# First attention of an encoder: one reciprocal for two blocks' sums, and a lower rate of filling products

## The chip, the cores and the metric

The kernel runs on one core of a Trainium2 chip. The metric is the device time of one execution in microseconds (us), from its first instruction to its last. Names of engines: PE is the matrix engine (PEld its weight load), DVE the vector engine, ACT the scalar engine, POOL the GpSimd engine, SP the engine that issues most DMAs. Lines such as L1004 are lines of the kernel before; the change's own lines stand in its diff.

## The reference, cut to what matters

A two-layer encoder over 512 tokens of width 1024, float32 throughout, is computed. The first layer's attention has two groups of eight heads; both use the same softmax attention:

```python
def one(qblk):                                  # a block of 128 queries
    sc = einsum('bkgqd,bksd->bkgqs', qblk, kt) * scale
    p = softmax(sc, axis=-1)
    return einsum('bkgqs,bksd->bkgqd', p, vt)
```

Group A has 64-wide queries and keys; group B has 96-wide ones that come from low-rank latents. Their outputs are joined and pass through one projection, then an MLP follows; the second layer has a neighbourhood attention and another MLP, then a final norm.

## The kernel before, in words

Float32 accuracy is had by splitting each operand into a high and a low part and adding three products (`mm3`, L500 to L503; two passes for group A's scores). So a weight chunk is loaded by SP (L190), copied to its high part by ACT (L212, L222) and its low part is made by DVE or POOL (L202).

The change lies in `attend` (L961 to L1022), which treats 16 heads of 4 blocks, thus 64 blocks of 128 queries, numbered 0 to 63 below. Blocks 0 to 31 are group A, 32 to 47 the first half of group B, 48 to 63 its second half. One block goes through these steps:

- scores: two (A) or three (B) matmuls of 128x512 into a PSUM bank `s`, of which there are two (L997);
- row maximum: a DVE instruction that writes the scaled scores to a tile `p` in SBUF, with the maximum in a column (L1001). There are five buffers `p`;
- exponential on ACT, with the sum of the row into another column (L1003);
- one reciprocal on DVE (L1004), and one scaling of `p` by it on POOL (L1005);
- three blocks later in program order: four transposes on PE into a bank `t`, of which there are two (L972), the copy of the high part by ACT (L974), and the low part by DVE (L975);
- for each two blocks: eight value matmuls (L985), four by the high parts and four by the low parts in turn. At a head's end ACT and DVE fold the two halves of the output (L946, L949), and for each two heads the result is split (L833 on ACT, L830 on DVE).

Between blocks `fill.run(1.5)` in `step` (L1088) emits other products, called filling products here: generators that each report an estimated duration (0.69 for an `mm3`), of which so many are emitted that 1.5 us more are used up. During group A these are the projections to the latents (L1090 to L1093), the latents' norm, and queries, keys and values of B's first half (`projB`, L838; L850, L878, and L907 to L909 for the values). From block 35 on they are parts of the output projection (L1084 to L1087) and B's second half. `fill.until` (L1044) emits all that is left of a half's projections before its first block, since that block reads them.

This gives the program's order only. The instructions of this stage are then ordered by a scheduler, which decides for each engine what comes first (the second layer's attention has an order written out by hand, the first has not). So a rate changed in one line moves rows on all engines.

## Time and profile before

| | |
|---|---|
| median of 3 runs | 1183.46 us (1182.31 to 1184.22) |
| profiled execution, first to last instruction | 1184.0 us |
| PE busy | 1160.5 us, 98% |
| DVE busy | 883.2 us, 75% |
| ACT busy | 640.3 us, 54% |
| POOL busy | 526.1 us, 44% |
| first scores of the stage that is changed | at 68.95 us |
| last transposes of the stage | at 247.17 us |

No time around the span is given for the profiled execution; its span lies among the three runs, 0.5 us over their median. A matmul's duration in the trace overlaps the next one's, so what one costs on PE is read from the start of one row to the start of the next. The same holds for DVE and ACT.

### The profile page before, as it was taken

The page shows a single profiled execution, that of the slowest core. Times are in us where ns is not written, and L with a number is a line of the kernel's source. Part 1 is how long each engine was busy: PE and PEld are TensorE (multiplying, and loading weights), DVE is VectorE, ACT ScalarE, POOL GpSimd, SP SyncE. Part 2 cuts the span into 40 slices and gives each one's busy share as a digit, 9 for nine tenths or more (in the row PEclk, how much of TensorE's full clock was granted, in tenths as well). Part 3 has the DMA queues.
Part 4 walks back from the last instruction along what each step waited for, and adds up shares of the span by engine and source line. Part 5 has one row for each costly group of instructions (what it writes and reads, how often), then busy time and mean ns, then how long its engine had stood idle before and what let it go on. Part 6 is the DMA issues. An engine that isn't in the chain of part 4 may idle for free.

```text
span 1184.0 us, 19784 instructions
## 1 busy us (share of the span) xinstructions
PE 1160.5 (98%) x7128; PEld 1021.2 (86%) x7128; DVE 883.2 (75%) x1514; ACT 640.3 (54%) x1081; POOL 526.1 (44%) x662
## 2 busy tenths in 40 slices
PE   9989999999999999999999999999999999999997
PEld 8667778888899899988998998988889989998895
DVE  5788998878967368786884676667996736778975
ACT  4468676664546247562553565555554624666344
POOL 3267343224562377819602232231376625774710
PEclk9999999999999999999999999999999999999998
DMA  7223225212524723225226464433352341322412
GB/s 244 71 54 92 68 78 134 62 56 77 167 86 134 263 70 90 72 90 165 67 72 178 131 184 126 116 112 109 107 165 76 115 134 55 98 64 89 143 36 71
DMA packets 110145, 128.01 MB, mean 108 GB/s; under 512 B 9075, under 2 KB 86816, under 8 KB 110048
## 3 DMA queue, kind: packets, MB, share of 16 engines
q1 hardware_dynamic: 106992, 119.30, 33.5%
q0 software_dynamic: 2304, 6.31, 2.2%
q8 instruction: 56, 0.92, 0.3%
q10 hardware_dynamic: 752, 1.15, 0.3%
q14 instruction: 41, 0.34, 0.1%
HBM read 104.32 MB, written 6.29 MB: 93 GB/s over the span
## 4 chain that ended last, share of the span: by engine, by line
PE 81%; DVE 4%; ACT 1%; issue 1%; POOL 0%; DVEq 0%; ACTq 0%
PE mm L503 8%; PE mm L501 8%; PE mm L502 8%; PE mm L390 4%; PE mm L389 4%; PE mm L388 4%; PE t L388 3%; PE t L389 3%; PE t L390 3%; PE s L502 2%; PE s L503 2%; PE s L501 2%; PE s L390 2%; PE s L388 2%; PE s L389 2%; PE s L997 2%
## 5 line engine op out<-in xcount | busy, mean ns | idle before, releaser
L309 DVE TENSOR_TENSOR wlo<-a,whi 128x896 fp32r<-128x896 f32 x132 | 161.8, 1230 | 83.7 <-ACT whi L308 82.9
L308 ACT ACTIVATE whi<-a 128x896 fp32r<-128x896 f32 x132 | 125.0, 950 | 155.0 <-PE o L502 45.8
L501 PE MATMUL mm<-a,whi 128*128 128x512 f32 x485 | 195.9, 406 | 0.9 <-DVE a L915 0.7
L503 PE MATMUL mm<-a,wlo 128*128 128x512 f32 x485 | 192.1, 397 | 2.5 <-DVE wlo L202 2.5
L502 PE MATMUL mm<-a,whi 128*128 128x512 f32 x485 | 192.5, 397 | 0.1
L202 DVE TENSOR_TENSOR wlo<-raw,whi 128x1024 fp32r<-128x1024 f32 (+4 forms) x117 | 139.3, 1193 | 66.4 <-ACT whi L212 63.9
L212 ACT ACTIVATE whi<-raw 128x1024 fp32r<-128x1024 f32 (+3 forms) x120 | 116.4, 971 | 92.2 <-PE s L502 39.8
L302 POOL TENSOR_TENSOR a<-a 128x128 f32<-128x128 f32 x132 | 85.1, 645 | 173.3 <-DMA a<-in_ffn_w_up_dram 103.9
L303 POOL TENSOR_TENSOR a<-a 128x256 f32<-128x256 f32 x132 | 120.2, 910 | 10.3
L304 POOL TENSOR_TENSOR a<-a 128x128 f32<-128x128 f32 x132 | 115.1, 872 | 10.3
L503 PEld LDWEIGHTS mm<-a,wlo 128*128 128x128 f32 x485 | 91.7, 189 | 23.7 <-DVE wlo L202 3.4
L501 PEld LDWEIGHTS mm<-a,whi 128*128 128x128 f32 x485 | 91.8, 189 | 20.4 <-PE t L972 0.9
L502 PEld LDWEIGHTS mm<-a,whi 128*128 128x128 f32 x485 | 91.9, 190 | 17.4 <-DVE a L545 0.4
L388 PE MATMUL mm<-a,whi 128*128 128x256 f32 x370 | 103.9, 281 | 0.0
L389 PE MATMUL mm<-a,whi 128*128 128x256 f32 x370 | 103.9, 281 | 0.0
L390 PE MATMUL mm<-a,wlo 128*128 128x256 f32 x370 | 103.7, 280 | 0.0
L1005 POOL TENSOR_SCALAR p<-p,ti 128x512 f32<-128x512 f32 x64 | 46.2, 724 | 92.3 <-DVE ti L1004 81.1
L1430 POOL TENSOR_SCALAR p<-p,ti 128x256 f32<-128x256 f32 x64 | 35.6, 567 | 104.8 <-DVE ti L1429 91.8
L388 PE MATMUL t<-a,whi 128*128 128x256 f32 x264 | 74.2, 281 | 0.0
L389 PE MATMUL t<-a,whi 128*128 128x256 f32 x264 | 74.1, 281 | 0.0
L390 PE MATMUL t<-a,wlo 128*128 128x256 f32 x264 | 73.9, 280 | 0.0
L390 PEld LDWEIGHTS mm<-a,wlo 128*128 128x128 f32 x370 | 69.6, 188 | 0.2 <-DVE wlo L309 0.2
(338 smaller groups left out, 3210.8 us busy)
## 6 DMA issues: line engine op xcount, KB each, us to landing
a<-in_ffn_w_up_dram SPq DMA_DIRECT2D x104, 256.0 KB
raw<-in_ffn_w_down_dram SPq DMA_DIRECT2D x46, 512.0 KB
raw<-in_od_w_qkv_dram SPq DMA_DIRECT2D x64, 128.0 KB
a<-in_ffn_w_down_dram SPq DMA_DIRECT2D x28, 256.0 KB
raw<-in_ffn_w_up_dram SPq DMA_DIRECT2D x12, 512.0 KB
raw<-in_ev_w_in_dram SPq DMA_DIRECT2D x12, 384.0 KB
a<-a SPq DMA_DIRECT2D x18, 256.0 KB
bias<-bx SPq DMA_DIRECT2D x16, 256.0 KB
```

The source lines that it names most:

```text
L202: z = lambda: (eng or DVE).tensor_tensor(to, src, f32(high), op=ALU.subtract)
L212: ACT.activation(hi[:, 0:m], raw[:, 0:m], AF.Copy)
L303: POOL.tensor_tensor(r[:, 4:6], r[:, 2:3].to_broadcast([P, 2, P]), r[:, 0:7:6], op=ALU.add)
L304: POOL.tensor_tensor(r[:, 7], r[:, 3], r[:, 5], op=ALU.subtract)
L308: ACT.activation(hi[:, 0:896], raw[:, 128:1024], AF.Copy)
L309: DVE.tensor_tensor(lo[:, 0:896], raw[:, 128:1024], f32(hi[:, 0:896]), op=ALU.subtract)
L388: PE.matmul(o, wh, x[:, 0], start=kp == 0 and n in (0, 1, 3, 5), stop=False, skip_group_check=True)
L389: PE.matmul(o, wh, x[:, 1], start=False, stop=False, skip_group_check=True)
L390: PE.matmul(o, wl, x[:, 0], start=False, stop=kp == self.np - 1, skip_group_check=True)
L501: PE.matmul(o, wh, xh, start=first, stop=False)
L502: PE.matmul(o, wh, xl, start=False, stop=False)
L503: PE.matmul(o, wl, xh, start=False, stop=last)
```

## The change

The diff, whole:

```diff
@@ scores, in attend @@
-            t = tiny(4)
+            z = i % 2
+            if z == 0:
+                h["two"] = tiny(8), []
+            t, ps_ = h["two"]
             p = pp.tile([P, 512], F32, tag="p", name=nm("p"))
+            ps_.append(p)
             DVE.tensor_tensor_reduce(p, s, zeros.to_broadcast([P, S]), op0=ALU.add, op1=ALU.min, scale=h["scale"](i),
-                                     scalar=3e38, accum_out=t[:, 1:2])
-            ACT.activation(p, p, AF.Exp, bias=t[:, 1:2], scale=-1.0, accum_out=t[:, 2:3])
-            DVE.reciprocal(t[:, 3:4], t[:, 2:3])
-            POOL.tensor_scalar(p, p, t[:, 3:4], 1.0, op0=ALU.mult, op1=ALU.mult)
+                                     scalar=3e38, accum_out=t[:, z : z + 1])
+            ACT.activation(p, p, AF.Exp, bias=t[:, z : z + 1], scale=-1.0, accum_out=t[:, 2 + z : 3 + z])
+            if z:
+                DVE.reciprocal(t[:, 4:6], t[:, 2:4])
+                for n, p_ in enumerate(ps_):
+                    POOL.tensor_scalar(p_, p_, t[:, 4 + n : 5 + n], 1.0, op0=ALU.mult, op1=ALU.mult)
             return p
@@ step @@
-        fill.run(1.5)
+        fill.run(1.25)
```

Blocks of one head are taken in pairs (0 and 1, 2 and 3). A pair has one tile of eight columns for its maxima, sums and reciprocals. The even block is no longer scaled behind its own exponential: one reciprocal of two columns stands behind the odd block's exponential, and then POOL scales both. The number of reciprocals falls from 64 to 32; all other instructions are the same in number. The rate of the filling products falls from 1.5 to 1.25 for each block (the `fill.run(1.5)` at L1022, behind the last block, stays).

What the scheduler makes of it is shown at three places. The first is DVE near the stage's beginning: L1001 is the row maximum (L1005 in the change), L1004 the reciprocal (L1009), L975 the low part of a transposed block; L508, L631 and L634 belong to the latents and to the rotation of queries. Before:

```order
L1001 ISA p_750,ti_749<-s_739,zeros,scA 128x512
L1001 ISA ti_749 128x1
L1004 RECIPROCAL ti_682<-ti_682 128x1
L1004 RECIPROCAL ti_697<-ti_697 128x1
L1001 ISA p_772,ti_771<-s_768,zeros,scA 128x512
L1001 ISA ti_771 128x1
L1004 RECIPROCAL ti_718<-ti_718 128x1
L975 TENSOR_TENSOR a_725<-t_726,a_724 128x4x128
L631 TENSOR_TENSOR sc_631<-sc_631,sc_622 128x512
L1004 RECIPROCAL ti_749<-ti_749 128x1
L975 TENSOR_TENSOR a_725<-t_755,a_724 128x4x128
```

and in the change, from the same block (number 4) on:

```order
L1005 ISA p_743,ti_742<-s_732,zeros,scA 128x512
L1005 ISA ti_742 128x1
L1009 RECIPROCAL ti_637<-ti_637 128x2
L1009 RECIPROCAL ti_692<-ti_692 128x2
L1005 ISA p_762,ti_742<-s_759,zeros,scA 128x512
L1005 ISA ti_742 128x1
L975 TENSOR_TENSOR a_712<-t_713,a_711 128x4x128
L634 TENSOR_TENSOR sc_736<-sc_631,a_621 128x512
L975 TENSOR_TENSOR a_712<-t_746,a_711 128x4x128
L1009 RECIPROCAL ti_742<-ti_742 128x2
L1005 ISA p_793,ti_792<-s_789,zeros,scA 128x512
```

The reciprocal for blocks 0 and 1 (`ti_637`) now stands behind the maximum of block 4; before, block 0's stood ahead of it. The rotation's L634 stands between the low parts of blocks 0 and 1.

The second place is PE for the same blocks: L997 is scores, L972 transposes, L985 values, L501 to L503 filling products. Before, from the scores of block 5 on:

```order
L997 MATMUL s_768<-a_129,a_609 128x512 x2
L972 MATMUL t_726<-cst,p_638 128x128 x4
L997 MATMUL s_810<-a_129,a_609 128x512 x2
L972 MATMUL t_755<-cst,p_683 128x128 x4
L997 MATMUL s_832<-a_129,a_609 128x512 x2
L503 MATMUL mm_1011<-a_114,wlo_801 128x512
L501 MATMUL mm_1011<-a_115,whi_800 128x512
L972 MATMUL t_779<-cst,p_698 128x128 x4
L985 MATMUL o_786<-a_724,a_131 128x256
L502 MATMUL mm_1011<-a_115,whi_800 128x512
L503 MATMUL mm_1011<-a_115,wlo_801 128x512
L501 MATMUL mm_1011<-a_116,whi_899 128x512
```

and in the change:

```order
L997 MATMUL s_759<-a_129,a_609 128x512 x2
L503 MATMUL mm_643<-a_121,wlo_723 128x512
L997 MATMUL s_789<-a_129,a_609 128x512 x2
L972 MATMUL t_713<-cst,p_638 128x128 x4
L972 MATMUL t_746<-cst,p_677 128x128 x4
L997 MATMUL s_815<-a_129,a_609 128x512 x2
L972 MATMUL t_770<-cst,p_693 128x128 x4
L985 MATMUL o_777<-a_711,a_131 128x256
L985 MATMUL o_777<-a_712,a_131 128x256
L985 MATMUL o_777<-a_711,a_131 128x256
```

Transposes of a pair stand together, and between them and the values no filling products are left. From the scores of block 5 to those of block 13 the whole order has 16 filling matmuls before and one in the change.

The third place is PE where group A ends, at the first scores of block 32. Before:

```order
L972 MATMUL t_1793<-cst,p_1704 128x128 x4
L972 MATMUL t_1812<-cst,p_1741 128x128 x2
L997 MATMUL s_1783<-a_1604,a_1528 128x512 x3
L997 MATMUL s_1800<-a_1604,a_1528 128x512 x3
L972 MATMUL t_1812<-cst,p_1741 128x128 x2
L985 MATMUL o_1819<-a_1762,a_131 128x256
L503 MATMUL mm_1878<-a_1003,wlo_1894 128x512
```

and in the change:

```order
L501 MATMUL mm_1843<-a_1549,whi_1861 128x512
L502 MATMUL mm_1843<-a_1549,whi_1861 128x512
L503 MATMUL mm_1843<-a_1549,wlo_1862 128x512
L501 MATMUL mm_1843<-a_1839,whi_1861 128x512
L502 MATMUL mm_1843<-a_1839,whi_1861 128x512
L997 MATMUL s_1751<-a_1693,a_1616 128x512 x3
L997 MATMUL s_1766<-a_1693,a_1616 128x512 x3
L503 MATMUL mm_1843<-a_1839,wlo_1862 128x512
L501 MATMUL mm_1844<-a_1549,whi_1861 128x512
L997 MATMUL s_1794<-a_1693,a_1616 128x512 x3
L997 MATMUL s_1809<-a_1693,a_1616 128x512 x3
L502 MATMUL mm_1844<-a_1549,whi_1861 128x512
```

Before, the last transposes and values of group A stand among the first scores of B. In the change all of A is done, 23 filling matmuls in a row follow, and only then come the scores of block 32. The same holds at block 48, with 13 in a row. Behind each of the two places few filling matmuls are left: 5 from the scores of block 32 to those of block 41 (36 before), and 7 from block 48 to block 57 (44 before).

## The prediction

> **What bounds the kernel now.** First comes the page's row for PE, then the table of busy time in five stretches of the stage that is changed (columns: stretch, its length, busy us of PE, PEld, DVE, ACT and POOL with their instructions, granted clock, share of DMA, GB/s), and one stretch of five microseconds:
>
> ```profile
> PE 1160.5 (98%) x7128; PEld 1021.2 (86%) x7128; DVE 883.2 (75%) x1514; ACT 640.3 (54%) x1081; POOL 526.1 (44%) x662
> 75.00:105.00 30.00, 29.07 (x165) 23.46 (x163) 25.60 (x68) 24.53 (x57) 19.33 (x22) 0.94 0.24 64
> 105.00:140.00 35.00, 33.78 (x188) 25.54 (x187) 29.82 (x78) 25.68 (x55) 19.93 (x22) 1.00 0.28 69
> 140.00:160.00 20.00, 18.56 (x119) 15.69 (x118) 19.66 (x47) 16.21 (x36) 4.21 (x7) 1.00 0.43 106
> 160.00:205.00 45.00, 44.78 (x266) 38.30 (x265) 39.41 (x87) 31.68 (x69) 19.17 (x23) 1.00 0.37 100
> 205.00:250.00 45.00, 44.78 (x264) 37.48 (x263) 36.02 (x82) 28.92 (x60) 11.11 (x16) 1.00 0.19 59
> 75.00:80.00 5.00, 5.00 (x18) 3.88 (x17) 3.29 (x12) 2.74 (x8) 0.74 (x2) 0.66 0.00 0
> ```
>
> PE sets the time: 98% of the span, and in the stage idle for 0.93, 1.22, 1.44, 0.22 and 0.22 us, together 4.03 us from 75 to 250. Its matmuls are the same in number after the change, so what the change can give is at most this idle time and what PE loses between kinds of rows. DVE is the next engine: 150.5 of these 175 us, and 19.66 of 20 from 140 to 160. The list of PE's waits from 60 to 255 says for whom it waited:
>
> ```profile
> PE s L997 <- DVE ti L1001: 2.9, 2, 2.4
> PE o L985 <- DVE a L975: 1.2, 3, 0.5
> PE mm L501 <- DVE a L915: 0.7, 1, 0.7
> PE t L530 <- DVE rsB L582: 0.6, 1, 0.6
> PE t L972 <- DVE ti L1004: 0.5, 2, 0.3
> ```
>
> All are waits for DVE, and only 0.5 us of them name the reciprocal. The 2.4 us of the first row lie at 72.2 to 74.6, ahead of the scores of block 2, where the order of PE is the same in both kernels; this one stays.
>
> **What a row costs.** From the timeline of PE (start, duration, what, and in brackets the wait ahead of it), start to start:
>
> ```profile
> 74.61 0.76 PE L997 MATMUL s<-a,a 128*128 128x512 f32 x2 [2.39 <-DVE ti L1001]
> 79.28 0.63 PE L997 MATMUL s<-a,a 128*128 128x512 f32 x2
> ...
> 84.41 0.60 PE L972 MATMUL t<-cst,p 128*128 128x128 f32 x4
> 84.77 0.48 PE L502 MATMUL mm<-a,whi 128*128 128x512 f32 x1
> 85.08 0.40 PE L503 MATMUL mm<-a,wlo 128*128 128x512 f32 x1
> 85.32 0.40 PE L501 MATMUL mm<-a,whi 128*128 128x512 f32 x1
> ...
> 94.03 0.99 PE L985 MATMUL o<-a,a 128*128 128x256 f32 x7
> 94.86 0.39 PE L997 MATMUL s<-a,a 128*128 128x512 f32 x1
> ...
> 95.99 0.63 PE L997 MATMUL s<-a,a 128*128 128x512 f32 x2
> 96.46 0.60 PE L972 MATMUL t<-cst,p 128*128 128x128 f32 x4
> ```
>
> A filling matmul costs 0.24 us (85.08 to 85.32), 0.08 more behind transposes (84.77 to 85.08); one block's transposes 0.36; a value matmul 0.83 / 7 = 0.119; a score matmul 0.47 / 2 = 0.235. From the scores of block 5 (79.28) to those of block 13 (95.99) the order of before has 16 score, 16 filling and 32 value matmuls and transposes of ten blocks: 7.5 + 3.8 + 3.6 = 14.9 us. The stretch took 16.7; the 1.8 us over are 33 changes from one kind of row to another, 0.055 us each.
>
> DVE, ACT and POOL in the same way:
>
> ```profile
> 80.50 0.75 DVE L1001 CUSTOM_DVE_ANT_0 p<-s,zeros,scA 128x512 f32<-128x512 f32 x1 [0.58 <-PE t L972]
> ...
> 83.97 0.82 DVE L634 TENSOR_TENSOR sc<-sc,a 128x512 fp32r<-128x512 f32 x1
> 84.72 0.68 DVE L975 TENSOR_TENSOR a<-t,a 128x512 fp32r<-128x512 f32 x1
> 85.32 0.15 DVE L1004 RECIPROCAL ti<-ti 128x1 f32<-128x1 f32 x1
> 85.39 0.72 DVE L1001 CUSTOM_DVE_ANT_0 p<-s,zeros,scA 128x512 f32<-128x512 f32 x1
> 86.05 0.68 DVE L975 TENSOR_TENSOR a<-t,a 128x512 fp32r<-128x512 f32 x1
> 86.65 0.73 DVE L508 SCALAR_TENSOR_TENSOR a<-mm,gT,a 128x512 fp32r<-128x512 f32 x1
> ...
> 88.59 0.68 DVE L949 TENSOR_TENSOR sc<-o,sc 64x512 f32<-64x512 f32 x1 [0.41 <-ACT sc L946]
> 89.22 0.69 DVE L975 TENSOR_TENSOR a<-t,a 128x512 fp32r<-128x512 f32 x1
> ```
>
> ```profile
> 97.36 0.59 ACT L974 ACTIVATE a<-t 128x512 fp32r<-128x512 f32 x1
> 97.84 0.72 ACT L1003 ACTIVATE p<-p,ti 128x512 f32<-128x512 f32 x1
> 98.45 0.20 ACT L1003 ACTIVATION_READ_ACCUMULATOR p<-p,ti 128x1 f32 x1
> ```
>
> ```profile
> 82.83 1.43 POOL L1005 TENSOR_SCALAR p<-p,ti 128x512 f32<-128x512 f32 x2 [0.71 <-DVE ti L1004]
> ```
>
> On DVE a row maximum costs 0.66, a low part 0.60, L634 0.75, a fold 0.63, and a reciprocal 0.07, though it is shown as 0.15. On ACT a copy of transposes costs 0.48, an exponential 0.61 and then its sum. POOL scales a block in 0.72.
>
> **The change, step by step.** *The reciprocals.* 32 fewer at 0.07 us are 2.2 us off DVE. PE waited 0.5 us for them, so by themselves they are worth at most that; on DVE they lie beside PE's work. A reciprocal of two columns isn't in the trace; between 0.07 (one column) and 0.14 (two reciprocals), I take 0.07. *The pair.* The even block is scaled one block later. From its scores' end: two maxima 1.3, an exponential with its sum about 0.7, the reciprocal, the scaling 0.7, and two low parts of older blocks that stand between on DVE 1.2: some 4.0 us, against 2.7 without the odd block's maximum and one low part. PE has three blocks of rows to cover it: at 0.47 + 0.36 + 4 x 0.119 = 1.31 each in group A that is 3.9 us, in B with a third score matmul 4.6. So the cover, which was ample, is just used up where no filling stands. *The rate.* It takes the filling from some places and heaps it at others, as the orders show, so there are such places.
>
> The Trainium skill (Perfetto Trace Analysis, Optimizing Scalar/DVE Operations) says that joining small operations helps an engine that is saturated, while for one that isn't but leaves bubbles elsewhere, breaking instructions up may let work end sooner. In this stage DVE is at 150.5 of 175 us and all of PE's waits are for it, so the second half of that rule speaks against the pair; by it the stage would be worth a loss, by the saved 2.2 us a gain.
>
> *First low stretch, blocks 5 to 13.* One filling matmul instead of 16, nine blocks of transposes, 25 value matmuls, 22 changes of kind: 4.0 + 3.2 + 3.0 + 1.2 = 11.4 us of PE. DVE must do, from the maximum of block 5 to the end of that of block 11 (two banks of scores let PE be no further ahead): seven maxima 4.6, seven low parts 4.2, three reciprocals 0.2, L634 0.75, a fold 0.63, thus 10.4, and it starts 1.2 behind PE (80.50 against 79.28): 11.6. The engines tie, so local waits show. The first one: blocks 0 and 1 are scaled behind the maximum of block 4, at about 79.7 and 80.4, so their transposes end near 80.2 and 80.9. DVE then has the maximum of block 5 (its `p` is block 0's, as in the row at 80.50), the low part of block 0, L634, and the low part of block 1: 80.2 + 0.66 + 0.60 + 0.75 + 0.60 = 82.8. PE has scores 7 (0.47), transposes 2 (0.36) and one value matmul until 81.9, and waits 0.9. Followed on, the values of blocks 2 and 3 wait 0.5 for the low part of block 3, and small pieces make 0.4: 1.8 us, between 0.9 (the first alone) and 3.0 (each of four pairs 0.75, half of the 1.43 that POOL needs for two). Before, the stretch to 105 had 0.93. **Term: +0.9.**
>
> *105 to 140.* The work there keeps its mix (the latents' chain, the rotation); 1.22 us of waits stay, from 0 to 2.4. A new wait can come in: tiles of eight columns are now shared by the pairs and the latents' norm, whose steps then wait for POOL's scaling, up to 1.43 us. The filling rows that stand between that norm's statistics and its broadcast (15 and a block's scores, 4.0 us) hide it. **Term: 0.**
>
> *The ends of group A and of B's first half.* The projections that the next heads read now end late. Their copies by SP (Q and K between partitions) move behind them, and the next scores behind those; 23 filling matmuls x 0.235 = 5.4 us cover a copy, for which the nearest row is
>
> ```profile
> a<-a POOLq DMA_DIRECT2D x16, 256.0 KB, 3.4
> ```
>
> At A's end the low-rank values are split behind block 29: on ACT three splits and a weight conversion stand ahead of the copy of block 31.
>
> ```profile
> L914 ACT ACTIVATE a<-mm,rsB 128x256 fp32r<-128x256 f32 x8 | 3.8, 476 | 1.2 <-DVE a L915 0.6 <-PE mm L909 0.5
> L222 ACT ACTIVATE whi<-raw 128x512 fp32r<-128x512 f32 x6 | 3.6, 625 | 0.0
> ```
>
> 3 x 0.48 + 0.62 + 2 x 0.48 = 3.0 us, against half a block of transposes, eight values, transposes and two filling matmuls on PE, 2.0: a wait of 1.0. Before, the same splits stood among full DVE work and PE idled 1.44 from 140 to 160. **Term: -0.4**, between -1.4 and +0.5. At B's middle seven rows more cover it: **+0.3**, between 0 and 1.0; there was nothing there before.
>
> *Second and third low stretch, blocks 32 to 41 and 48 to 57.* PE 1.54 a block, DVE 0.66 + 0.60 + 0.04 + 0.63 / 4 = 1.46, so PE leads by little. The loss per block lies between 0 and the 0.22 of the first stretch (1.8 over eight); nearest is before's own start of B, 160 to 205 with 0.22 in all. I take 0.05: **+1.0** for 20 blocks, from 0 to 4.4.
>
> *Changes of kind.* Over the stage the orders have 261 before and 241 now: 20 x 0.055 = **-1.1**; by the transposes' ends alone (66 to 58, 0.08 each) -0.6.
>
> Sum: 0.9 + 0 - 0.4 + 0.3 + 1.0 - 1.1 = +0.7 us. On the profiled 1184.0 that is 1184.7, on the median, 0.5 under it, 1184.2.
>
> **Rivals.** *Slower: the pair's scaling comes too late wherever filling is missing.* At each pair of the 28 blocks in low stretches (8, 10 and 10) PE would come to the even block's transposes before POOL has scaled it. It decides whether PE reaches them within the 4.0 us worked out above; with 3.9 to 4.6 us of cover this is near. At 0.5 a pair, 14 pairs lose 7.0 instead of 1.8 + 1.0: 1184.2 + 4.2 = 1188.4. For it speaks that DVE ties with PE, against it that PE may run two blocks ahead.
>
> *Faster: the waits are gone.* DVE with 2.2 us less may never be last; only the first 0.9 us remains of the 4.03: 1183.46 - 4.03 + 0.9 - 1.1 = 1179.2. For it speaks that from 140 to 160 DVE was full and that the work there is now spread; against it, the shown order of L634.
>
> *One more slow phase of the clock.* The gap of 2.39 us in the row at 74.61 was followed by 0.66 of the clock from 75 to 80, 1.7 us lost. If one new wait grows from 0.9 to 2.3, that is 1.4 + 1.7 more: 1187.3. The Trainium skill (TensorE: Matmul & The Clock Gate, What's actually happening) puts the price at an idle window of about 3.4 us; by that rule this rival falls away, but the row here had only 2.4.
>
> *It does not spread anything.* The order shows already that filling is bunched (23 and 13 in a row); this is in the forecast.
>
> **How the numbers follow.** The forecast, small terms that nearly cancel, 0.40; the late scaling 0.30; the clock 0.06; the waits gone 0.24. 0.2% (2.4 us) is about what a measurement can tell from no change. The forecast's lies within it; the first two rivals are slower, the third faster. The range, 1180.0 to 1189.0, takes in most of both sides; the forecast's own is 1181.5 to 1186.0.
>
> **What would show it.** Right: PE idle by 1 to 2 us from 75 to 92, with values waiting for L975, the stage's end within 2 us of 247.2, 32 reciprocals of 0.07 start to start. Wrong: transposes that wait for POOL in most pairs behind 150 (late scaling), a second stretch of lower clock, or PE idle under 2 us in all from 75 to 250 (faster). It would also be wrong if rows beyond the stage changed in time, since their order there is the same.

## The result, and the profile after

The change made the kernel slower: 1191.59 us (1190.79 to 1191.99, 4 runs) against 1183.72 us of before beside it (1182.31 to 1184.22, 4 runs), a ratio of 1.0067 (95% interval 1.0053 to 1.0082). The prediction, 1184.2 us with a range up to 1189.0, was wrong. In the profiled executions the span grew from 1184.0 to 1189.3 us. A recorded time is about 2.0 us longer than its span (1191.29 against 1189.3 for the profiled execution of the change), so the profiled execution of before took some 1186 us and was not, as the working had it, 0.5 us over the median, but some 2.5. Its trace holds one phase of half clock more than that of the change (below), which is in part why the spans differ by less than the medians.

The page's row for PE and the others, and the same five stretches of the stage (columns as before: stretch, its length, busy us of PE, PEld, DVE, ACT and POOL, granted clock, share of DMA, GB/s), of the changed kernel:

```profile
PE 1162.2 (98%) x7128; PEld 1019.9 (86%) x7128; DVE 881.2 (74%) x1482; ACT 639.9 (54%) x1081; POOL 526.2 (44%) x662
75.00:105.00 30.00, 28.05 (x155) 21.74 (x154) 25.20 (x58) 24.79 (x57) 17.01 (x20) 0.95 0.21 54
105.00:140.00 35.00, 32.32 (x176) 24.28 (x175) 27.38 (x67) 22.92 (x51) 20.71 (x22) 1.00 0.25 67
140.00:160.00 20.00, 19.64 (x130) 16.44 (x129) 18.52 (x42) 17.20 (x36) 5.95 (x8) 1.00 0.31 67
160.00:205.00 45.00, 44.10 (x250) 36.79 (x249) 37.27 (x79) 30.87 (x67) 17.73 (x23) 1.00 0.34 94
205.00:250.00 45.00, 44.48 (x257) 36.25 (x255) 35.74 (x78) 30.23 (x64) 11.06 (x15) 1.00 0.32 90
```

DVE has 32 instructions and 2.0 us less, as meant, and from 140 to 160 it is no longer full. But PE is now idle for 1.95, 2.68, 0.36, 0.90 and 0.52 us, together 6.41 instead of 4.03: most of the new idle time is in group A, from 75 to 140. The list of PE's waits from 60 to 255 in the changed kernel (L1005 is the row maximum there, L1009 the reciprocal, L1011 the scaling; the other lines of the stage kept their numbers):

```profile
PE s L997 <- DVE ti L1005: 2.7, 2, 2.4
PE s L997 <- DMA a<-sc: 1.9, 3, 0.9
PE o L985 <- DVE a L975: 1.8, 4, 0.9
PE s L997 <- DVE a L624: 1.4, 1, 1.4
PE t L972 <- POOL p L1011: 1.1, 3, 0.5
PE o L985 <- DVE a L915: 0.8, 1, 0.8
PE o L985 <- ACT a L974: 0.2, 1, 0.2
```

Two releasers are new in PE's rows: SP's copies of the rotated queries (`a<-sc`) and POOL's scaling. The places of the copies, of the longest wait for a low part and of the stage's end, from PE's timeline of the changed kernel:

```profile
86.48 0.50 PE L997 MATMUL s<-a,a 128*128 128x512 f32 x1 [0.48 <-DMA a<-sc]
...
106.50 1.18 PE L997 MATMUL s<-a,a 128*128 128x512 f32 x4 [0.86 <-DMA a<-sc]
...
120.00 1.09 PE L985 MATMUL o<-a,a 128*128 128x256 f32 x7 [0.94 <-DVE a L975]
...
126.10 0.73 PE L997 MATMUL s<-a,a 128*128 128x512 f32 x2 [0.54 <-DMA a<-sc]
...
252.45 0.60 PE L972 MATMUL t<-cst,p 128*128 128x128 f32 x4
```

The waits for a DMA stand ahead of the scores of blocks 8, 16 and 24, where a new pair of heads begins. The last row is the last of the stage's transposes, at 247.17 before: the stage ends 5.3 us later, of which PE's idle time shows only 2.4. More of it stands in the list of the weight loads' waits, first of before, then of the changed kernel:

```profile
PEld o L985 <- DVE a L975: 4.3, 11, 1.0
...
PEld t L972 <- POOL p L1005: 1.3, 4, 0.5
...
PEld o L985 <- ACT a L974: 0.8, 4, 0.2
```

```profile
PEld t L972 <- POOL p L1011: 5.6, 14, 0.9
...
PEld o L985 <- DVE a L975: 4.7, 12, 1.1
PEld o L985 <- ACT a L974: 3.9, 11, 1.2
```

A weight load that waits while PE still drains older matmuls makes no idle time of PE in the records, yet the next matmul begins later than it could. The transposes' loads waited 4 times for POOL before and 14 times after.

So idle time is too small a measure here. A better one is the **loss**: the time from the start of one of PE's matmuls to the start of the next, less a price for the first of them (0.23 us with 512 columns, 0.1165 with 256, 0.0885 with 128, all near the steps that the prediction read), summed from the first scores of block 0 on. A step counts with the matmul that it leads to, so the 1.5 us ahead of block 0 are in every column, and the wait ahead of a block's first scores is in the next one. It holds waits of both kinds, changes of kind, and slow phases of the clock. Up to a block's first scores, and to the stage's last value matmul, in us:

| kernel (profiled execution) | block 4 | 8 | 14 | 16 | 24 | 32 | 48 | end |
|---|---|---|---|---|---|---|---|---|
| before | 5.5 | 7.1 | 8.1 | 9.7 | 12.6 | 17.3 | 20.4 | 23.3 |
| the change | 5.5 | 8.9 | 11.7 | 12.1 | 16.0 | 22.0 | 25.4 | 29.1 |

Of 5.8 us, 4.7 are lost by block 32, the end of group A, and 3.6 already by block 14. Steps between two matmuls that are over 0.2 us too long make 14.8 us (23 of them) after, 10.8 (16) before; the rest of the difference sits in small ones, nearly all of them where PE goes from one kind of row to another.

Beyond the stage two things differ, which together nearly cancel. The 400 matmuls 2400 to 2800 of PE, in the first MLP, took 47.8 us before and take 49.2 now. And in the matmuls 6400 to 6800, at about 1100 us, a phase of half clock is missing (66.2 us, before 67.7). 5.3 + 1.4 - 1.5 = 5.2 of the 5.3 us by which the spans differ.

### The profile page after: what moved, and what is told of

It reads as the page before. It is cut to its first block, busy times and chain, and to the rows that moved or that the text cites. A ratio compares the mean times of both kernels' runs of the same rounds, so it can differ in the third digit from the quotient of the medians.

```text
span 1189.3 us, 19718 instructions
## 1 busy us (share of the span) xinstructions
PE 1162.2 (98%) x7128; PEld 1019.9 (86%) x7128; DVE 881.2 (74%) x1482; ACT 639.9 (54%) x1081; POOL 526.2 (44%) x662
## 4 chain that ended last, share of the span: by engine, by line
PE 86%; DVE 7%; ACT 2%; DMA 2%; POOL 1%; issue 1%; SPq 0%; DVEq 0%; POOLq 0%; ACTq 0%
PE mm L501 8%; PE mm L503 8%; PE mm L502 8%; PE mm L390 3%; PE mm L388 3%; PE mm L389 3%; PE s L502 3%; PE s L501 3%; PE s L503 3%; PE t L388 2%; PE t L389 2%; PE t L390 2%; PE s L997 2%; PE s L388 2%; PE s L389 2%; PE s L390 2%
## 5 line engine op out<-in xcount | busy, mean ns | idle before, releaser
L501 PE MATMUL mm<-a,whi 128*128 128x512 f32 x485 | 195.1, 404 | 0.2 <-DVE hT L931 0.2
L503 PE MATMUL mm<-a,wlo 128*128 128x512 f32 x485 | 191.4, 396 | 2.7 <-DVE wlo L202 2.7
L202 DVE TENSOR_TENSOR wlo<-raw,whi 128x1024 fp32r<-128x1024 f32 (+4 forms) x117 | 138.9, 1191 | 66.2 <-ACT whi L212 65.9
L503 PEld LDWEIGHTS mm<-a,wlo 128*128 128x128 f32 x485 | 91.1, 188 | 23.5 <-DVE wlo L202 3.6
L501 PEld LDWEIGHTS mm<-a,whi 128*128 128x128 f32 x485 | 91.4, 189 | 20.4 <-issue 1.4
L1011 POOL TENSOR_SCALAR p<-p,ti 128x512 f32<-128x512 f32 x64 | 46.2, 733 | 92.6 <-DVE ti L1009 82.0
```

What stands on the lines that cost most here:

```text
L202: z = lambda: (eng or DVE).tensor_tensor(to, src, f32(high), op=ALU.subtract)
L501: PE.matmul(o, wh, xh, start=first, stop=False)
L503: PE.matmul(o, wl, xh, start=False, stop=last)
```

## Experiments

There were sixteen runs of fourteen kernels, in four groups; each group shares its runs of before. Medians of before were 1184.77, 1184.63, 1184.18 and 1184.00 us. Two theories were to be told apart for the pair: that it scales the first block too late, and that the edit only shuffles the scheduler's order. For the rate there were two as well: that filling is missing where PE needs it in group A, and that the queries' copies come late.

A table first, which the readings below use. "Filling" counts the matmuls in PE's rows that are neither scores nor transposes of blocks nor values, from block 5 to 13, 24 to 32, 41 to 48 and 48 to 57 (the texts written ahead of the runs count two or so fewer in the heaps). Since a phase of half clock falls in some executions and not in others, the last column is the mean time of those runs alone whose mean granted clock was 0.996 (number of runs in brackets).

| kernel | filling | median us (runs) | ratio, 95% interval | us at clock 0.996 |
|---|---|---|---|---|
| before | 16, 58, 70, 44 | 1184.0 to 1184.8 | 1 | 1184.3 (72) |
| the change | 1, 124, 91, 7 | 1191.59 (4) | 1.0067, 1.0053 to 1.0082 | 1191.0 (2) |
| pair_150 | 20, 51, 70, 44 | 1187.04 (11) | 1.0024, 1.0016 to 1.0033 | 1186.4 (5) |
| pair_150b, the same | 20, 51, 70, 44 | 1188.74 (7) | 1.0035, 1.0023 to 1.0047 | 1186.8 (2) |
| pairA_150 | 20, 51, 70, 44 | 1184.55 (11) | 0.9998, 0.9989 to 1.0007 | 1184.7 (4) |
| pairB_150 | 16, 61, 70, 44 | 1183.50 (11) | 0.9990, 0.9981 to 0.9999 | 1184.1 (4) |
| tiny8_150 | 16, 61, 70, 44 | 1183.50 (11) | 0.9990, 0.9981 to 0.9999 | 1182.4 (4) |
| join2_150 | 20, 50, 70, 44 | 1187.22 (11) | 1.0024, 1.0015 to 1.0033 | 1186.8 (7) |
| late2_150 | 16, 52, 70, 44 | 1182.67 (10) | 0.9979, 0.9968 to 0.9990 | 1182.2 (1) |
| late2_150b, the same | 16, 52, 70, 44 | 1182.41 (11) | 0.9983, 0.9973 to 0.9993 | 1182.5 (6) |
| single_125 | 6, 121, 92, 7 | 1190.45 (5) | 1.0048, 1.0036 to 1.0060 | 1189.2 (2) |
| late2_125 | 6, 124, 92, 7 | 1189.17 (5) | 1.0036, 1.0024 to 1.0048 | 1189.2 (2) |
| rot_125 | 7, 124, 91, 7 | 1192.91 (6) | 1.0071, 1.0056 to 1.0085 | 1192.0 (2) |
| rateA_125 | 6, 121, 70, 44 | 1187.78 (12) | 1.0026, 1.0017 to 1.0036 | 1187.5 (6) |
| rateA1_125 | 6, 80, 70, 44 | 1190.32 (6) | 1.0043, 1.0028 to 1.0057 | 1190.1 (3) |
| rateB_125 | 16, 58, 92, 7 | 1183.37 (12) | 0.9997, 0.9986 to 1.0007 | 1183.5 (7) |
| lead2_125 | 25, 37, 92, 7 | 1189.26 (8) | 1.0039, 1.0025 to 1.0053 | 1187.4 (1) |
| single_175 | 25, 18, 68, 45 | 1187.45 (12) | 1.0020, 1.0011 to 1.0030 | 1186.2 (2) |

### The two halves of the change, each alone

**pair_150** is the change with the rate back:

```diff
-        fill.run(1.25)
+        fill.run(1.5)
```

> The pair alone, with the filling rate left at 1.5. Theory F (filling): the loss comes from the lower rate, which takes the filling from blocks 5 to 13, 32 to 41 and 48 to 57; with the old rate the order has 20, 35 and 44 filling matmuls there (16, 36 and 44 before), so the time is 1182 to 1185.5 us, ratio 0.999 to 1.0015. Rival P (pair): the even block's late scaling makes transposes wait for POOL wherever they stand; then 1187 to 1192 us, ratio 1.003 to 1.007, and PE waits for POOL about as in the changed kernel (1.1 us shown idle, 5.6 us ahead of weight loads). Rival O (any new order costs some us by chance): any ratio from 0.997 to 1.007.

**single_125** is the kernel before with the new rate:

```diff
-        fill.run(1.5)
+        fill.run(1.25)
```

> The rate of 1.25 alone, with one reciprocal and one scaling for each block as before. The order has 6, 7 and 7 filling matmuls in blocks 5 to 13, 32 to 41 and 48 to 57. Theory F: 1188 to 1193 us, ratio 1.004 to 1.008, with PE losing 2 us or more by block 14 against the kernel before. Rival P: 1183 to 1186 us, ratio 0.9995 to 1.002, since no scaling is late. If both parts cost, it lies between, and the two parts' losses add up to 7.9 us.

Measured were 1187.04 us (ratio 1.0024) and 1190.45 us (1.0048). Both halves cost, the rate about twice what the pair does, and their sum, 0.72%, is within the interval of the whole, 0.67% (a second run of the pair alone, pair_150b below, gave 1.0035).

### Where the rate costs

Two kernels put the rate of 1.25 on one group alone, on before: **rateA_125** has

```diff
-        fill.run(1.5)
+        fill.run(1.25 if n < 32 else 1.5)
```

> Rate 1.25 for blocks 0 to 31 alone, 1.5 after; single reciprocals. Filling matmuls in blocks 5 to 13, 16 to 24 and 24 to 32: 6, 23 and 119 (16, 53 and 58 before); from block 41 on as before. Theory F with the place that the traces so far show (group A, where a block has the least PE work and PE meets DVE, ACT and the queries' copies): nearly the whole loss of the low rate, 4 to 6 us, 1188.5 to 1191 us, ratio 1.0035 to 1.005. If the heaps at blocks 31 and 47 are what costs, half of it: 1187 to 1188 us.

and **rateB_125** has

```diff
-        fill.run(1.5)
+        fill.run(1.5 if n < 32 else 1.25)
```

> Rate 1.5 for blocks 0 to 31 and 1.25 after; single reciprocals. Filling in blocks 32 to 41 and 48 to 57 falls to 27 and 7 (36 and 44 before), and is heaped at block 47; group A is as before. If group A is the place: at most 1 us over the kernel before, 1184 to 1186 us. If low stretches in B cost as those in A do (0.2 us or more a block): 1186.5 to 1188 us.

1187.78 us and 1183.37 us: in group B alone the lower rate costs nothing that can be measured, though the second half of B then has 7 filling matmuls instead of 44 in blocks 48 to 57. In group A alone it costs 0.26%, about half of single_125's 0.48%; that is the time that the text ahead of the run gave to the heaps at blocks 31 and 47. So the cost shows in A, but the two groups don't add up to the whole, and what is missing (1.7 us at equal clock) stays open. **rateA1_125** narrows the place to the first sixteen blocks (`1.25 if n < 16 else 1.5`):

> The kernel before with the filling rate at 1.25 in blocks 0 to 15 alone and 1.5 behind them: 6 filling matmuls instead of 16 stand in blocks 5 to 13, and 80 instead of 58 in blocks 24 to 31 (122 with 1.25 in all of group A, which took 1187.78 us). Theory F (what costs is that filling is missing in blocks 5 to 13): all of that loss, 1186.8 to 1188.0 us, the cumulative loss at the start of block 14 about 2.4 us over before. Rival P (what costs is the filling piled up in blocks 24 to 31, where changes of kind and waits grow): 1184.5 to 1186.0 us.

It took 1190.32 us, no less than the lower rate everywhere, and more than in all of group A. So the lower rate in the first half of A is enough, and the heap of 121 matmuls in blocks 24 to 32, of which this kernel has only 80, isn't needed. Its loss grew by 4.8 us from block 4 to 14 (5.56 to 10.35), that of before by 2.6; but from block 16 to 24 it also grew by 5.1 against 3.0, and from 24 to 32 by 6.9 against 4.7. PE's waits from 60 to 255 in this kernel:

```profile
PE o L985 <- DVE a L975: 3.0, 5, 0.9
PE s L997 <- DVE ti L1001: 2.4, 1, 2.4
PE s L997 <- DVE a L624: 1.4, 1, 1.4
PE s L997 <- DMA a<-sc: 1.2, 1, 1.2
PE mm L907 <- DVE a L830: 0.9, 1, 0.9
```

The values wait for DVE's low parts (3.0 us, before 1.2), the scores for the queries' copy, and a filling matmul for its operand. The expectation's bound of 1188.0 was passed by 2 us: the later loss, too, moves with what is emitted early. How, stays open, and so does why lowering the rate in fewer blocks cost some 2 us more than lowering it in all of A.

Two kernels put more filling early. **lead2_125** is the change with

```diff
-        fill.run(1.25)
+        fill.run(1.75 if n < 16 else 1.25)
```

> The changed kernel (pairs, 1.25) with a rate of 1.75 for blocks 0 to 15 only. Filling in blocks 5 to 13 is 25 (1 in the change, 16 before), in 16 to 24 69 (26), so that none of group A is poor in it; B as in the change. Theory F: PE's loss up to block 14 falls from 11.7 us (change) to 8 to 8.7, and the time to 1185.5 to 1188 us, though the pairs stay. Rival P (late scaling of pairs costs in itself): the loss falls by less than half, and it stays above 1188.5 us.

**single_175** is before with `fill.run(1.75)`:

> Single reciprocals and a rate of 1.75 throughout: filling in blocks 5 to 13 25, 16 to 24 93, but 24 to 32 only 18, so the poor stretch moves to the end of group A, where DVE splits the queries and keys of B. Theory F (what matters is that no stretch is poor, not that the rate is high): within 2 us of the kernel before with PE's loss moved from the blocks ahead of 16 to those from 24 to 32. If more filling early is better throughout: 1181 to 1183 us.

1189.26 us (1.0039) and 1187.45 us (1.0020). In the first stretch both did what missing filling foretells: with 25 filling matmuls in blocks 5 to 13 the loss from block 4 to 14 was 3.3 and 2.3 us (before: 2.6, the change: 6.2). But the time followed in part only: lead2_125 stayed over the 1185.5 to 1188 us that missing filling foretold, and single_175 is 2.4 us over before by the ratio, just beyond the 2 us foretold for it. The loss came back later, its largest single step ahead of the scores of block 16 (PE's timeline, lead2_125, then single_175):

```profile
111.21 0.85 PE L997 MATMUL s<-a,a 128*128 128x512 f32 x2 [2.80 <-DMA a<-sc]
```

```profile
109.20 0.70 PE L997 MATMUL s<-a,a 128*128 128x512 f32 x2 [1.77 <-DMA a<-sc]
```

Blocks then run ahead of the rotation of the next heads' queries, whose copies by SP end late. In lead2_125 a step of half clock follows this wait, 1.7 us more. But from block 16 to 24 lead2_125 lost 8.0 us and single_175 9.2, before 3.0, so the wait for the copy isn't all. Loss and, in brackets, filling in three stretches of group A:

| kernel | blocks 4 to 14 | 16 to 24 | 24 to 32 |
|---|---|---|---|
| the change | 6.2 (5) | 3.9 (26) | 6.0 (124) |
| rateA_125 | 5.0 (11) | 3.7 (23) | 6.0 (121) |
| rateA1_125 | 4.8 (11) | 5.1 (47) | 6.9 (80) |
| before | 2.6 (21) | 3.0 (55) | 4.7 (58) |
| lead2_125 | 3.3 (36) | 8.0 (71) | 2.8 (37) |
| single_175 | 2.3 (36) | 9.2 (95) | 0.4 (18) |

In the first stretch the loss falls as filling grows, up to 21 matmuls. Behind it that isn't so: single_175 was expected to lose from block 24 to 32, where it has least filling, and lost 0.4 us there; it lost most where its filling is heaped. In that heap filling matmuls waited 1.0 us for their own operands from DVE. So a stretch with little filling isn't dear by itself; the rate moves the loss from one place to another, and the runs don't separate what filling hides from what it costs.

**rot_125** asks about the copies from the other side. It is the change with the queries' sums emitted two blocks earlier:

```diff
-                if e == 1 and t < 3 and i == 0:
+                if e == 0 and t < 3 and i == 2:
```

> The changed kernel with the rotated queries of the next two heads made two blocks earlier (sum_q behind block 2 of the even head, not behind block 0 of the odd one); filling is 7, 5 and 7 in the three stretches, thus nearly as in the change. In the changed kernel the scores of blocks 8, 16 and 24 wait for the DMA of these queries (1.9 us shown). Theory R (the next queries come too late when filling is missing): those waits go, 1189 to 1190.5 us, 1 to 2.5 us faster than the changed kernel. Theory F without R: PE then waits for DVE instead, since DVE and PE tie there, and the time stays within 1 us of 1191.6.

It took 1192.91 us (1.0071), not less than the change. Its waits of PE from 60 to 255:

```profile
PE t L972 <- POOL p L1011: 3.2, 6, 1.0
PE s L997 <- DVE ti L1005: 2.7, 2, 2.4
PE o L985 <- DVE sc L949: 2.3, 2, 2.0
PE s L997 <- DVE a L624: 1.4, 1, 1.4
PE o L985 <- DVE a L915: 0.8, 1, 0.8
PE s L997 <- DMA a<-sc: 0.5, 1, 0.5
```

The waits for the copies did shrink, from 1.9 to 0.5 us, but POOL's scalings (1.1 to 3.2) and a fold (L949) came late instead. The late copies are not a cause that could be taken away alone here: other waits took their place.

### What the pair costs

**late2_125** is the change with two reciprocals of one column, each ahead of its own scaling, in place of the joined one; both still stand behind the second block's exponential in the program:

```diff
-                DVE.reciprocal(t[:, 4:6], t[:, 2:4])
                 for n, p_ in enumerate(ps_):
+                    DVE.reciprocal(t[:, 4 + n : 5 + n], t[:, 2 + n : 3 + n])
```

> The change with two reciprocals of one column in place of one of two, both behind the odd block's exponential: 64 reciprocals again, scaling as late as in the change. If joining the reciprocals is worth anything by itself (2.2 us of DVE by my sum), this is 0.5 to 2 us slower than the changed kernel: 1192 to 1194 us. If it is hidden beside PE, the same within 1 us: 1190.5 to 1192.5.

1189.17 us, under both of the expected ranges: no slower than single_125, and at equal clock 1.8 us under the change (two runs each). So at this rate it isn't the later place in the program that costs. The same at the old rate, **late2_150**, stood beside three kernels: **tiny8_150**, before with nothing altered but the tile's width,

```diff
-            t = tiny(4)
+            t = tiny(8)
```

and **pairA_150** and **pairB_150**, with the pairs of the change in blocks 0 to 31 or 32 to 63 alone (`two` is `count[0] < 32` or `count[0] >= 32`), both at the rate of 1.5:

```diff
+            two = count[0] < 32
             z = i % 2
-            if z == 0:
+            if z == 0 or not two:
                 h["two"] = tiny(8), []
...
-            if z:
+            if not two:
+                DVE.reciprocal(t[:, 4 + z : 5 + z], t[:, 2 + z : 3 + z])
+                POOL.tensor_scalar(p, p, t[:, 4 + z : 5 + z], 1.0, op0=ALU.mult, op1=ALU.mult)
+            elif z:
                 DVE.reciprocal(t[:, 4:6], t[:, 2:4])
```

> The change with two reciprocals of one column in place of the one of two columns, both scalings still behind the second block's sum, and the filling rate back at 1.5. It has one DVE instruction per pair more than the run with pairs at 1.5 (1187.04 us), and the scalings as late. Theory L: 1186.5 to 1188 us, the ratio near 1.0025. If the joined reciprocal itself costs (its result frees both tiles together): as before, 1184 to 1185. Theory S: anywhere within 3 us of these.

> The kernel before with one thing altered: the small tile of a block has eight columns instead of four; every instruction is as before, but the scheduler's order near blocks 15 to 40 shifts by a few rows. Theory L (a later scaling is what the pair costs): nothing is later, so 1183.7 to 1185.5 us, a ratio within 0.1% of 1. Theory S (any edit that shifts the scheduler's order moves the time by some 2 us, and the pair's 0.24% is no more than that): off by 1.5 us or more to either side, with nothing to say which. For the first MLP (matmuls no. 2400 to 2800 behind the start: 47.8 us before, 49.0 with pairs): if the tile's size, and so where tiles lie in memory, costs the 1.2 us there, they are here too; if it is the pairing, 47.7 to 48.2.

> The change with the filling rate back at 1.5, and the pairs in group A alone (blocks 0 to 31); blocks 32 to 63 have one reciprocal and one scaling each. Theory L with its place in group A: 1186.5 to 1187.5 us, a ratio near 1.002 as with pairs everywhere, transposes waiting for POOL's scaling at some 86, 104 and 153 us, and the loss up to block 32 near 1.0 us over before. If pairs cost the same everywhere: 1185.5 to 1186. In the first MLP 49.0 us if the loss there belongs to pairs in A or to the wider tile.

> The change with the filling rate back at 1.5, and the pairs in group B alone (blocks 32 to 63); blocks 0 to 31 have one reciprocal and one scaling each, as before. Theory L with its place in group A: 1183.5 to 1185.5 us, a ratio within 0.1% of 1. If pairs cost the same everywhere: 1185.5 to 1186.5. Theory S: within 2 us of before on either side. In the first MLP 47.8 us if the loss there belongs to pairs in A, 49.0 if it belongs to pairs in B or to the wider tile.

Against before none of the four is slower, and two reciprocals are 0.2% faster than before; pairA_150 and late2_150 came out under what was expected of late scaling (1186.5 to 1187.5 and to 1188). That looked as if pairs cost nothing, against pair_150's 1.0024. An answer is in tiny8_150: **the tile's width alone shifts the scheduler's order**, and that order is 1.9 us better at equal clock (0.10% by all runs). The loss from block 24 to 32, 4.7 us before, is 2.0 in tiny8_150. Why the scheduler chooses otherwise stays open. Measured against tiny8_150, which shares the tile, pairs in A cost 2.3 us, in B 1.7, both 4.0 to 4.4, and two reciprocals nothing. The order is shared in part only: with pairs in A the stretch from block 24 to 32 has 51 filling matmuls instead of 61 and loses 4.5 us again. So both theories have a share, some 4 us for the pair and 2 back from a shuffled order, but this comparison can't say how much of the 4 is order.

The last step tells more. **join2_150** is pair_150 with the joined reciprocal issued twice; the second block is scaled by the second copy:

```diff
                 DVE.reciprocal(t[:, 4:6], t[:, 2:4])
+                DVE.reciprocal(t[:, 6:8], t[:, 2:4])
                 for n, p_ in enumerate(ps_):
-                    POOL.tensor_scalar(p_, p_, t[:, 4 + n : 5 + n], 1.0, op0=ALU.mult, op1=ALU.mult)
+                    POOL.tensor_scalar(p_, p_, t[:, 4 + 3 * n : 5 + 3 * n], 1.0, op0=ALU.mult, op1=ALU.mult)
```

> The change at the old filling rate of 1.5, with the two-column reciprocal of a pair issued twice: the first block is scaled by the first copy, the second block by the second. So 64 reciprocals instead of 32, as in the run with two reciprocals of one column, but each of them waits for the sums of both blocks. Theory W (what costs is that the first block's scaling waits for the second block's sum): as pairs at 1.5, within 1.5 us of that run beside it, its even blocks scaled some 3.6 us behind their exponential. Theory N (the number and kind of the reciprocals counts): as the run with two reciprocals at 1.5, 1182.0 to 1184.0 us. Theory S (only the scheduler's order scatters): anywhere within 3 us.

> The change at the old filling rate of 1.5, once more, now on one chip with its counterparts. Theory W: 1186.0 to 1188.0 us against 1184.2 to 1184.8 of before, and at least 3 us above the run with two reciprocals. If the halves measured before (pairs in group A alone 0.9998, in group B alone 0.9990) are all that there is, and the earlier 1.0024 was the chip's: 1183.5 to 1185.0.

> The change at the old rate of 1.5 with two one-column reciprocals in place of the joined one, once more, now beside the joined one on one chip. Theory W: 1182.0 to 1184.0 us, its even blocks scaled 2.1 us behind their exponential against 3.6. If the earlier 0.9979 was the chip's: 1184 to 1187.

1187.22, 1188.74 and 1182.41 us, on one chip. join2_150 has as many reciprocals as late2_150b and takes 4.8 us more; it differs in that each of them needs both blocks' sums. Neither the number of instructions nor the chip explains that; the orders are close (50 and 52 filling matmuls from block 24 to 32), though not the same. Of the difference, 3.5 us are loss up to the stage's end, 0.6 lie in the first MLP, and a phase of half clock, which only the profiled execution of join2_150 has at 1100 us, makes the profiles differ further. From the end of a block's exponential to the end of its scaling, as a mean over 32 blocks of the profiled executions:

| kernel | first block of a pair | second | blocks of A scaled less than 1 us ahead of PE's transposes |
|---|---|---|---|
| before | 1.74 us | 1.68 us | 3 of 32 |
| late2_150b | 2.11 | 1.70 | 6 |
| pair_150b | 3.54 | 2.29 | 10 |
| join2_150 | 3.62 | 2.41 | 11 |
| the change | 3.79 | 2.43 | 12 |

One pair, near the end of group A, shows it row by row. PE, DVE, ACT and POOL in pair_150b; L1007 is the second block's exponential:

```profile
148.99 0.72 ACT L1007 ACTIVATE p<-p,ti 128x512 f32<-128x512 f32 x1
...
149.24 0.71 PE L997 MATMUL s<-a,a 128*128 128x512 f32 x2
...
149.62 0.19 ACT L1007 ACTIVATION_READ_ACCUMULATOR p<-p,ti 128x1 f32 x1
...
149.87 0.74 DVE L1005 CUSTOM_DVE_ANT_0 p<-s,zeros,scA 128x512 f32<-128x512 f32 x1
...
150.53 0.16 DVE L1009 RECIPROCAL ti<-ti 128x2 f32<-128x2 f32 x1
...
150.61 0.67 DVE L975 TENSOR_TENSOR a<-t,a 128x512 fp32r<-128x512 f32 x1
...
150.86 1.36 POOL L1011 TENSOR_SCALAR p<-p,ti 128x512 f32<-128x512 f32 x2 [5.34 <-DVE ti L1009]
...
151.61 0.66 PE L972 MATMUL t<-cst,p 128*128 128x128 f32 x4 [0.88 <-POOL p L1011]
```

The sum is read at 149.81. But DVE's next place in its order is the following block's maximum, and the reciprocal comes behind it, at 150.53. POOL had been idle for 5.34 us, and PE waits 0.88. The same place in late2_150b:

```profile
149.61 0.72 ACT L1007 ACTIVATE p<-p,ti 128x512 f32<-128x512 f32 x1
...
149.80 0.72 PE L997 MATMUL s<-a,a 128*128 128x512 f32 x2
...
150.03 0.15 DVE L1010 RECIPROCAL ti<-ti 128x1 f32<-128x1 f32 x1
...
150.24 0.19 ACT L1007 ACTIVATION_READ_ACCUMULATOR p<-p,ti 128x1 f32 x1
...
150.38 1.36 POOL L1011 TENSOR_SCALAR p<-p,ti 128x512 f32<-128x512 f32 x2 [4.97 <-DVE ti L1010]
...
150.60 0.40 PE L502 MATMUL mm<-a,whi 128*128 128x512 f32 x1
...
151.12 0.66 PE L972 MATMUL t<-cst,p 128*128 128x128 f32 x4
```

The first block's reciprocal stands ahead of the second's sum. From the start of the same scores to POOL's first scaling it is 0.58 us here and 1.62 there. PE shows no idle time; from start to start (150.60 to 151.12) it lost 0.29 us, against 0.88 of idle time there. late2_150 is also the fastest version that was run, 0.2% under before and, by the two ratios, 0.9% under the change; since tiny8_150 at equal clock is as fast (1182.4), its gain over before is most likely that of a shifted order.

### The first MLP

The 400 matmuls there took 48.6 to 49.4 us in all seven profiled kernels that join the sums in group B (the change, pair_150, pair_150b, join2_150, rot_125, lead2_125, pairB_150), and 47.7 to 48.5 in the eleven others; the two sets are only 0.1 us apart. The order of every engine beyond the stage is the same in before and the change, and in tiny8_150 and pairB_150. What PE and POOL waited for from 440 to 500, in before and then in the changed kernel:

```profile
POOL a L302 <- DMA a<-in_ffn_w_up_dram: 2.3, 6, 0.8
```

```profile
POOL a L302 <- DMA a<-in_ffn_w_up_dram: 3.8, 5, 1.3
...
PE mm L390 <- DVE wlo L309: 0.7, 1, 0.7
PE s L390 <- DVE wlo L309: 0.5, 1, 0.5
```

POOL waits 1.5 us longer for a weight transfer, and PE 1.2 us for low parts of weights that DVE makes behind it. Why this is so in just these kernels stays open: the tile's width isn't it (tiny8_150 48.1 us), nor are pairs in A (pairA_150 48.1).

## Why the prediction was wrong, point by point

- **What bounds.** Right: PE. Not all of its waits were for DVE, as the working says: the list of before also has one of 0.2 us for POOL, and new ones came from POOL, ACT and SP's copies. Wrong in the measure: idle time of PE rose by 2.4 us, the stage by 5.3. Waits of weight loads and small steps hold the rest, and the working had no term for them.
- **The reciprocals.** Right in size: 32 of them, and one of two columns costs 0.08 us start to start (150.53 to 150.61), between the bounds given. They were worth nothing: doubling them in join2_150 changed nothing (1187.22 against 1187.04 and 1188.74).
- **The pair.** The working gave the first block's scaling 4.0 us from its scores' end against a cover of 3.9 and called that "just used up where no filling stands"; measured, the delay behind the exponential grew by 2.05 us (1.74 to 3.79). What failed is the price: no term of its own was given to it at the places where filling does stand. With the old rate it cost 2.1 to 2.5 us over before at equal clock, and 4.0 to 4.4 over the kernel with the same tile. The rival of late scaling, 0.30, named the mechanism; its time of 1188.4 lies between pair_150 and the change.
- **The first low stretch, +0.9: the step that failed.** The place was right, the size was not. From the scores of block 5 to those of block 13 the working gives 11.4 + 1.8 = 13.2 us, 14.4 at its upper bound; it took 15.6 (78.33 to 93.95), with just the rows that the working counts. Over the price of its matmuls the stretch lost 5.7 us and before 2.1: 3.6 more instead of 0.9. PE's idle time there, 1.9 us, is near the 1.8 of the working, but only 0.5 of it is for low parts. What had no term are the weight loads' waits (from 78 to 96 they waited 5.6 us for POOL, DVE, ACT and a copy, before 1.5) and the first of the three waits for copies of the queries. From block 4 to 14 rateA1_125, with the rate alone, lost 2.2 us more than before, of the change's 3.6; the rate explains the larger part, and the pair at the old rate only 0.3 (pair_150). The other 1.1 us come with both together, where 5 filling matmuls are left in these blocks instead of rateA1_125's 11; what each of them would cost alone at 5 is not known.
- **105 to 140, 0.** Wrong: idle there went from 1.22 to 2.68. The two waits for copies at 106.50 and 126.10 and one for a low part at 120.00 are in it.
- **The end of A, -0.4.** Right in sign where it was looked for: from 140 to 160 PE's idle time fell from 1.44 to 0.36. But over the blocks 24 to 32, which the changed kernel treats from 126 to 168, the loss rose from 4.7 to 6.0.
- **B's middle, +0.3, and the second and third low stretch, +1.0.** Too dear for the rate: lowered in B alone (rateB_125) it didn't change the time (0.9997), which fits the working's 1.54 us of PE against 1.46 of DVE a block. In the change itself the loss from block 32 on grew by 1.1 us.
- **Changes of kind, -1.1.** Wrong. There were fewer (248 before, 224 after, with scores, transposes, values and all else as four kinds and steps up to 0.2 us over), but what they lost together rose from -0.5 to 1.1 us. So 0.055 us a change, taken from one stretch, isn't a price that is saved when the change goes; small waits for operands in these steps are the likely reason, not shown one by one. Over the whole stage the loss grew by 5.8 us where the terms add up to 0.7: 3.6 up to block 14, 1.0 from there to block 32, 1.1 behind it.
- **One more slow phase of the clock.** Didn't come in the changed kernel's profiled execution; it did in lead2_125's, behind the wait of 2.80 us. It is a matter of position, below.
- **Waits gone, 0.24.** Fell: from 140 to 160 they went, as the rival said, and came back from 75 to 140.
- **What would show it.** From 75 to 92 PE was idle by 1.6 us, with values waiting for L975 among other waits, so this sign spoke for the forecast though more time was lost beside it. The stage's end (252.45, not within 2 us of 247.2) spoke against it. Of the signs of late scaling, PE's own list has three waits for POOL in all, one of them behind 150 (0.28 us at 154.94); the weight loads' list has 14, nine of them behind 150, which would have been the list to name. Rows beyond the stage did change in time, the last sign: the 400 matmuls in the first MLP took 1.4 us more, in the same order.
- **The Trainium skill** (Perfetto Trace Analysis, Optimizing Scalar/DVE Operations) advises to break up instructions where an engine isn't saturated but leaves bubbles elsewhere. The runs agree: two instructions instead of one joined took 1182.41 against 1188.74 us.

## What to carry to other kernels

An instruction that is joined over two blocks waits for the later of their inputs, and everything behind it waits as well; here 0.07 us saved per instruction was no return for some 2 us of delay of the first block. When independent work that fills an engine's gaps is spread differently, look at the place where it gets thin and at the place where it is heaped, since loss turned up at both, and count waits of weight loads and copies as well as idle time: here idle time showed less than half of the loss. And where a scheduler sets the order, an edit that changes nothing in the work (a tile of eight columns) moved the time by 1.9 us at equal clock, so a half of a change is to be compared with a kernel whose order is as near as can be had.

## What the hardware showed that was not expected

Phases of half clock ahead of the end of the program last 3.413 us, and they begin on a fixed grid of that step within an execution: between the granted clock's records lie 68.267, 1023.998 and 71.680 us in before, 20, 300 and 21 steps. Whether a gap of PE is followed by one depends on how it falls on the grid. In the 18 profiles there are 39 gaps of PE over 1.5 us, near 74, 110, 123 and 1105 us. With 1.93 us or more of a gap inside one step (25 of them, from 1.93 to 2.80) the next step ran at half clock; with 1.89 or less (14, from 1.09 to 1.89) none did, though twelve of these gaps were over 1.93 us long in all. No other step ahead of the last stretch of half clock had more than 1.89 us of idle time, small gaps added up. So the same wait of 2.4 us ahead of block 2's scores halved the clock in pair_150 and not in the same kernel run as pair_150b, from 73 to 78 us:

```profile
73.00:78.00 5.00, 4.09 (x12) 3.29 (x13) 3.59 (x9) 3.09 (x8) 0.00 (x0) 0.66 0.00 0
```

```profile
73.00:78.00 5.00, 4.63 (x20) 3.44 (x21) 3.89 (x13) 4.01 (x11) 0.82 (x2) 1.00 0.00 0
```

In pair_150 1.99 us of the gap lay in one step, in pair_150b 1.45 and 0.93 in two. The Trainium skill (TensorE: Matmul & The Clock Gate, What's actually happening) has an idle window of about 3.4 us. That is the length of the step here, but 1.93 us of idle time within it were enough; the runs decide. A step at half clock costs half of its 3.413 us, 1.7, and the spread among runs of one kernel goes with it: late2_150b took 1180.0 us at a mean clock of 0.997 (2 runs) and 1183.9 at 0.995 (3 runs). This is why the last column of the table holds the clock fixed.
